# A hybrid encoder block: a second tile for the row of forget logs, second key copies read from PSUM, and four gate chunks moved from the forgetting attention into the dense stage

## The chip, the cores and the metric

The kernel runs on one core of a Trainium2 chip. The metric is the device time of one execution in microseconds, and a kernel is judged by the median of its runs. TensorE (PE) multiplies; VectorE (DVE), ScalarE (ACT) and GpSimd (POOL) do the element-wise work; SyncE (SP) and POOL issue the DMAs. PSUM, into which TensorE writes, has eight banks, one for each 128 x 512 float32 tile here.

## The reference

One residual block over 1024 tokens of width 1024, in float32: a normalization, one input projection split among three token mixers, sigmoid gates for each mixer and channel, an output projection; then a second normalization and a convolutional GLU. Cut to what matters here:

```python
z = rmsnorm(x, norm_mix_g) @ w_in
hq, hf, hi, hg, fq, fk, fv, ff, mq, gate_logits = split(z)
y_a = hgrn2(hq, hf, hi, hg)              # 4 heads, chunkwise recurrence
y_b = fox(fq, fk, fv, ff)                # forgetting attention, 8 heads of 64
y_c = cross_attention(mq, mem)           # 4 heads of 128, 256 memory tokens
gates = sigmoid(gate_logits)             # 3 branches x 1024 channels
merged = sum(gates[b] * (y[b] @ w_br[b]) for the three branches)
x = x + merged @ w_out
x = x + conv_glu(rmsnorm(x, norm_ffn_g))

def fox(q, k, v, f_logit):               # for each head
    Fc = cumsum(log_sigmoid(f_logit + f_bias))       # the row of forget logs
    s = rmsnorm(q) . rmsnorm(k) / 8 + Fc[t] - Fc[s]  # s <= t, blocks of 128 queries
    return softmax(s) @ v
```

## The kernel before

Every float32 product is made of three float32r products of a high and a low part (`mm3`, L112: high x high, high x low, low x high). The high part is a rounded copy (`cast`, on ACT), the low part the difference (on DVE); `split` does both.

The normalized input stands in SBUF by channels as `uh` and `ul` (8 tiles each). It is multiplied with the input weights in three ways:

- *Chunk by chunk* (`cm_chunk`, L154): 128 output channels by 1024 tokens, in two halves of 512, each 8 x 3 matmuls into one bank `pp`.
- *Two chunks at once* (`dense_unit`, L450): a Strassen-like scheme over blocks of 512 tokens and half of the depth, with sums of weight blocks (`s1` to `s4`) and sums of input blocks prepared once (`T1` to `T4`). Seven products of 4 x 3 matmuls give both chunks. `PAIRS` lists the pairs of chunks: first the four query chunks of the memory attention (12 to 15), then gate chunks.
- *Token by token block* (`token_major`, L580): 128 tokens by about 256 channels, where `uh` is the stationary side. It makes keys, queries and values for attention (`fox_proj`, `fox_values`) and the HGRN inputs (`hgrn_values`).

There are 24 gate chunks (3 branches x 8), in the order `ORDER`. Two are made while the input arrives, `NCOVER` = 2 before the dense units, `NPAIR` = 10 in the dense units, and the rest one by one during the attention by `gates_early`: `NFOX` says how many beside each of the first seven heads. A gate chunk is multiplied by the norm's factor into a `gt` tile (`gate`, L379; three `gt` tiles rotate), goes through a tanh, and is stored to DRAM (`gd`) by a DMA on SP. The branches fetch it from there later.

The forgetting attention runs by pairs of heads (`fox_proj`, `fox_prep`, then `fox_attn` for the first and for the second head):

- `fox_proj(p)` writes the tokens' keys and queries to `z`, squares them (`fsq`), sums, takes the power -1/2 on POOL and multiplies.
- `fox_prep(p)` (L736) transposes `z` on TensorE into a bank `ptr` and leaves the high and low parts of keys and queries in 64 of 128 partitions, and the keys a second time in the other 64, since one product has the high query in one half and the low query in the other. ACT makes the high part `kh`, DVE the low part `kl`; POOL copies both into the other half.
- `fox_attn(p, i)` (L771) loads the head's row of forget logs to all partitions (`nf`, one tile). For each 128 queries (`tb`, 0 to 7) TensorE makes the logits in `lg` banks; DVE adds the forget logs and takes the maximum (L800), after POOL has added the mask for the diagonal block (`nfm`, L789); ACT takes the exponential (L810); POOL divides (L812). The probabilities lie in `pt`, four tiles of 1024 columns that rotate, and `fsq` takes a turn among them. By pairs of `tb`, TensorE transposes the probabilities, ACT and DVE split them (`ph`, `pl`), and TensorE multiplies with the values into `po`; the two parts of the result are added in `yp` (L838, one tile) and stored by a DMA on SP.

The program is woven: `weave` advances several generators by their shares. The first head of pair `p` is woven with the projection of the next pair; the second with the gate chunks of `NFOX`; the last pair with `hgrn_values`. Attention instructions have a priority 300 instructions ahead (`ahead`, `AHEAD`). A planner then orders each engine's instructions, with its own estimate of their times; a tile of a rotating tag waits for the last use of the tile that it takes over, in the order of the program. After the last head comes the HGRN stage: `hgrn_prep` (L903) makes three chunks for a head, for the first head through `gt` tiles (L914), and `hgrn_mix` runs the recurrence.

Of the kernel before, what the change touches and what calls it, by code (L numbers as in the profile page):

```python
# [8 lines left out]
F32 = mybir.dt.float32  # L9
F32R = mybir.dt.float32r  # L10
AF = mybir.ActivationFunctionType
ALU = mybir.AluOpType
AX = mybir.AxisListType

P = 128
T = 1024
# [9 lines left out]


ORDER = [(br, j) for br in (1, 0, 2) for j in range(8)]
NCOVER, NPAIR = 2, 10
NFOX = [0, 3, 0, 3, 0, 3, 1]  # L30

_dense = [12, 13, 14, 15] + [16 + 8 * br + j for br, j in ORDER[4:4 + NPAIR]]
PAIRS = list(zip(_dense[0::2], _dense[1::2]))
# [37 lines left out]
def tile_block(ctx: ExitStack, tc: tile.TileContext, xT, memT, x_rows, mem_rows, vec, fbias, mats, hmask, w_cm, w_hi, w_fqk, w_fv,  # L71
# [46 lines left out]
    def cast(eng, out, in_):  # L118
        if eng is S:
            return S.copy(out, in_)  # L120
        elif eng is V:
            V.tensor_copy(out, in_)
        else:
            G.tensor_scalar(out, in_, 1.0, 0.0, ALU.mult, ALU.add)
# [251 lines left out]
    def gate_tile():  # L376
        return home["pool"].tile([P, HB], F32, tag="gt", name="gt", bufs=3)
# [221 lines left out]
    pools = {}  # L599
# [114 lines left out]
    def fox_proj(p):  # L714

        fox_z[p] = [None, None]

        def evac(tb, ps):
            n, b = tb // 4, tb % 4
            if b == 0:  # L720
                fox_z[p][n] = pq.tile([P, 4, 256], F32, tag="z", name=f"z{p}_{n}", bufs=2)
            z = fox_z[p][n]
            S.activation(z[:, b, :], ps, AF.Copy, scale=rt[:, tb:tb + 1])
            if b == 3:
                zz = z.rearrange("p b (h d) -> p (b h) d", d=64)
                sq = pools["pf"].tile([P, 16, 64], F32, tag="pt", name="fsq", bufs=4) if p else \
                    pm.tile([P, 16, 64], F32, tag="fsq", name="fsq")
                r = pq.tile([P, 16], F32, tag="fr", name="fr", bufs=2)
                S.activation(sq, zz, AF.Square)
                V.reduce_sum(r, sq, axis=AX.X)  # L730
                rstd_small(r, r, 64)
                V.tensor_mul(zz, zz, r.unsqueeze(2).to_broadcast([P, 16, 64]))

        yield from token_major(w_fqk[p], 256, evac)

    def fox_prep(p, after=None):  # L736
        kh = [pf.tile([P, T], F32R, tag=f"kh{i}", name=f"kh{i}_{p}", bufs=1 + i) for i in range(2)]
        qa = [pf.tile([P, T], F32R, tag=f"qa{i}", name=f"qa{i}_{p}", bufs=1 + i) for i in range(2)]
        kl = [pf.tile([P, T], F32R, tag=f"kl{i}", name=f"kl{i}_{p}", bufs=1 + i) for i in range(2)]
        for n in range(2):  # L740
            sl = slice(n * HB, (n + 1) * HB)
            z = fox_z[p][n]
            for what in range(2):
                gc = col(C_FK) if what == 0 else fqs
                ptr = ps_tr()
                with tc.issue_after(after.ins) if after is not None else nullcontext():
                    for b in range(4):
                        PE.transpose(ptr[:, b * P:(b + 1) * P], z[:, b, what * P:(what + 1) * P], ident)
                for i in range(2):
                    a = slice(64 * i, 64 * i + 64)  # L750
                    o = slice(64 * (1 - i), 64 * (1 - i) + 64)
                    if what == 0:
                        S.activation(kh[i][a, sl], ptr[a, :], AF.Copy, scale=gc[a, :])
                        V.scalar_tensor_tensor(out=kl[i][a, sl], in0=ptr[a, :], scalar=gc[a, :],
                                               in1=kh[i][a, sl].bitcast(F32), op0=ALU.mult, op1=ALU.subtract)
                        cast(G, kh[i][o, sl], kh[i][a, sl].bitcast(F32))
                        cast(G, kl[i][o, sl], kl[i][a, sl].bitcast(F32))
                    else:
                        S.activation(qa[i][a, sl], ptr[a, :], AF.Copy, scale=gc[a, :])
                        V.scalar_tensor_tensor(out=qa[i][o, sl], in0=ptr[a, :], scalar=gc[a, :],  # L760
                                               in1=qa[i][a, sl].bitcast(F32), op0=ALU.mult, op1=ALU.subtract)
        fox_sets[p] = [kh, kl, qa, None]
# [8 lines left out]
    def fox_attn(p, i):  # L771
        kh, kl, qa, _ = fox_sets[p]
        h = 2 * p + i
        a = slice(64 * i, 64 * i + 64)
        if h not in fox_vh:
            fox_vsplit(h)
        vhl = fox_vh[h]
        nf = pf.tile([P, T], F32, tag="nf", name="nf")
        SP.dma_start(nf, negFd[h:h + 1, :].partition_broadcast(P))
        for tp in range(4):  # L780
            pts = []
            for j in range(2):
                tb = 2 * tp + j
                ns = (tb + 1) * P
                tsl = slice(tb * P, (tb + 1) * P)
                pt = pf.tile([P, T], F32, tag="pt", name="pt", bufs=4)
                st = pf.tile([P, 4], F32, tag="st", name="st", bufs=4)
                nfm = pf.tile([P, P], F32, tag="nfm", name="nfm")
                G.tensor_tensor(nfm, nf[:, tsl], mskf, ALU.add)  # L789
                m = 0  # L790
                for s0 in range(0, ns, HB):
                    w = min(HB, ns - s0)
                    ps = ps_lg()
                    PE.matmul(ps[:, :w], qa[i][:, tsl], kh[i][:, s0:s0 + w], start=True, stop=False)  # L794
                    fox_sets[p][3] = PE.matmul(ps[:, :w], qa[i][:, tsl], kl[i][:, s0:s0 + w], start=False, stop=True)  # L795

                    d = w - P if s0 + w == ns else w
                    for lo, hi, bias in ((0, d, nf[:, s0:s0 + d]), (d, w, nfm)):
                        if lo < hi:
                            V.tensor_tensor_reduce(out=pt[:, s0 + lo:s0 + hi], in0=ps[:, lo:hi], in1=bias,  # L800
                                                   op0=ALU.add, op1=ALU.max, scale=1.0, scalar=-3e38,
                                                   accum_out=st[:, m:m + 1])
                            m += 1
                if m == 3:
                    V.tensor_tensor(st[:, 0:1], st[:, 0:1], st[:, 2:3], ALU.max)
                if m > 1:
                    V.tensor_scalar(st[:, 2:3], st[:, 0:1], st[:, 1:2], -1.0, ALU.max, ALU.mult)  # L807
                else:
                    V.tensor_scalar(st[:, 2:3], st[:, 0:1], -1.0, None, ALU.mult)
                S.activation(pt[:, :ns], pt[:, :ns], AF.Exp, bias=st[:, 2:3], accum_out=st[:, 3:4])  # L810
                V.reciprocal(st[:, 3:4], st[:, 3:4])  # L811
                G.tensor_scalar(pt[:, :ns], pt[:, :ns], st[:, 3:4], 0.0, ALU.mult, ALU.add)  # L812
                pts.append(pt)
                yield
            po = ps_po()
            for sp in range(tp + 1):
                ptr = ps_tr()
                w = 384 if sp == tp else 512
                for jj in range(2):
                    sb = 2 * sp + jj  # L820
                    ssl = slice(sb * P, (sb + 1) * P)
                    if sb <= 2 * tp:
                        PE.transpose(ptr[:, jj * 256:jj * 256 + P], pts[0][:, ssl], ident)
                        PE.transpose(ptr[:, jj * 256 + P:jj * 256 + 256], pts[1][:, ssl], ident)  # L824
                    else:
                        PE.transpose(ptr[:, 256:384], pts[1][:, ssl], ident)
                ph = pf.tile([P, HB], F32R, tag="ph", name="ph", bufs=2)
                pl = pf.tile([P, HB], F32R, tag="pl", name="pl", bufs=2)
                split(S, ph[:, :w], pl[:, :w], ptr[:, :w])
                for jj in range(2):  # L830
                    sb = 2 * sp + jj
                    last = sb == 2 * tp + 1
                    o = po[:, P:256] if last else po[:, 0:256]
                    src = slice(256, 384) if last else slice(jj * 256, jj * 256 + 256)
                    PE.matmul(o, vhl[:, sb, :], ph[:, src], start=(sb == 0), stop=False)  # L835
                    PE.matmul(o, vhl[:, sb, :], pl[:, src], start=False, stop=last)  # L836
                yield
            yp = pf.tile([64, 256], F32, tag="yp", name="yp")  # L838
            S.copy(yp, po[64:128, :256])
            V.tensor_add(yp, po[0:64, :256], yp)  # L840
            SP.dma_start(ybd[a, p, tp * 256:(tp + 1) * 256], yp)
            yield
# [812 lines left out]
```

## Time and profile before

| | us |
|---|---|
| median of 3 runs | 1734.2 |
| lowest and highest | 1732.5, 1734.95 |
| the profiled execution's own time | 1735.67 |
| its span, first to last instruction | 1733.9 |
| TensorE busy | 1714.0 |
| VectorE busy | 1144.5 |
| ScalarE busy | 808.3 |
| GpSimd busy | 322.8 |

The rows below come from the page of the profile and from views of its trace. A group is one line, engine and operation with its tiles (out<-in) and its count, then busy time, mean duration in ns, idle time of the engine just before it and what ended most of that. A row of the timeline has the start in us from the span's start, the duration, engine, line and operation. Matmuls are pipelined and their ends are modelled, so the pace of TensorE is read from starts, not from durations. PEld is the loading of weights, which overlaps. PEclk is the TensorE clock that was granted, as a share of full speed.

### The profile page before, as it was taken

The page shows a single profiled execution, that of the slowest core. Times are in us where ns is not written, and L with a number is a line of the kernel's source. Part 1 is how long each engine was busy: PE and PEld are TensorE (multiplying, and loading weights), DVE is VectorE, ACT ScalarE, POOL GpSimd, SP SyncE. Part 2 cuts the span into 40 slices and gives each one's busy share as a digit, 9 for nine tenths or more (in the row PEclk, how much of TensorE's full clock was granted, in tenths as well). Part 3 has the DMA queues.
Part 4 walks back from the last instruction along what each step waited for, and adds up shares of the span by engine and source line. Part 5 has one row for each costly group of instructions (what it writes and reads, how often), then busy time and mean ns, then how long its engine had stood idle before and what let it go on. Part 6 is the DMA issues. An engine that isn't in the chain of part 4 may idle for free.

```text
span 1733.9 us, 24255 instructions
## 1 busy us (share of the span) xinstructions
PE 1714.0 (99%) x8941; PEld 1452.6 (84%) x8941; DVE 1144.5 (66%) x2046; ACT 808.3 (47%) x1436; POOL 322.8 (19%) x417
## 2 busy tenths in 40 slices
PE   8999999999999999999989999999999999999998
PEld 6778899989898998888878888788888888888887
DVE  7656545665666564886856745987777787765654
ACT  8634346645454553776531333644334344433332
POOL 0100022443433331544210000211111111100000
PEclk9999999999999999999999999999999999999999
DMA  9533142221212111100336542565445345494772
GB/s 358 179 123 115 66 137 86 76 90 44 98 62 79 55 50 56 61 31 24 111 113 199 162 182 97 158 172 168 138 148 140 116 133 152 159 348 157 249 264 85
DMA packets 83207, 227.23 MB, mean 131 GB/s; under 512 B 9600, under 2 KB 12424, under 8 KB 83088
## 3 DMA queue, kind: packets, MB, share of 16 engines
q1 hardware_dynamic: 65040, 161.19, 26.8%
q0 software_dynamic: 18048, 64.50, 12.8%
q8 instruction: 70, 1.15, 0.3%
q14 instruction: 49, 0.40, 0.1%
HBM read 180.78 MB, written 67.93 MB: 143 GB/s over the span
## 4 chain that ended last, share of the span: by engine, by line
PE 96%; DMA 2%; DVE 1%; SPq 0%; issue 0%; ACT 0%; POOL 0%; DVEq 0%; POOLq 0%; ACTq 0%
PE pp L116 21%; PE pp L115 21%; PE pp L114 21%; PE lg L116 4%; PE lg L115 4%; PE lg L114 4%; PE tr L115 2%; PE tr L116 2%; PE tr L114 2%; PE po L836 1%; PE lg L795 1%; PE lg L794 1%; PE po L835 1%; PE po L116 1%; PE po L114 1%; PE po L115 1%
## 5 line engine op out<-in xcount | busy, mean ns | idle before, releaser
L116 PE MATMUL pp<-uh,wl 128*128 128x512 f32 x412 | 164.4, 399 | 0.0
L115 PE MATMUL pp<-ul,wh 128*128 128x512 f32 x412 | 164.4, 399 | 0.0
L114 PE MATMUL pp<-uh,wh 128*128 128x512 f32 x412 | 163.6, 397 | 0.0
L115 PE MATMUL pp<-wl,uh 128*128 128x256 f32 (+1 forms) x512 | 145.9, 286 | 0.0
L116 PE MATMUL pp<-wh,ul 128*128 128x256 f32 (+1 forms) x512 | 145.6, 285 | 0.0
L114 PE MATMUL pp<-wh,uh 128*128 128x256 f32 (+1 forms) x512 | 145.1, 285 | 0.0
L120 ACT CAST wh<-s 128x512 fp32r<-128x512 f32 x113 | 68.3, 619 | 157.7 <-PE pp L115 84.9
L120 ACT CAST wh<-raw 128x1024 fp32r<-128x1024 f32 (+2 forms) x76 | 67.6, 890 | 111.6 <-PE pp L115 95.5
L120 ACT CAST wh<-rw 128x512 fp32r<-128x512 f32 x87 | 53.2, 619 | 104.7 <-PE pp L115 62.1
L1300 POOL DMA_DIRECT2D rw<-in_w_up x44 | 24.2, 556 | 399.4 <-DVE wl L1193 178.4
L114 PEld LDWEIGHTS pp<-wh,uh 128*128 128x128 f32 x512 | 96.7, 189 | 1.2
L116 PEld LDWEIGHTS pp<-wh,ul 128*128 128x128 f32 x512 | 96.8, 189 | 0.9
L115 PEld LDWEIGHTS pp<-wl,uh 128*128 128x128 f32 x512 | 96.7, 189 | 0.9
L128 DVE TENSOR_TENSOR wl<-raw,wh 128x1024 fp32r<-128x1024 f32 (+2 forms) x75 | 78.1, 1041 | 28.8 <-ACT wh L120 28.3
L120 ACT CAST dwh<-wr 128x1024 fp32r<-128x1024 f32 (+1 forms) x41 | 40.1, 979 | 118.5 <-PE tr L115 39.7
L114 PEld LDWEIGHTS pp<-uh,wh 128*128 128x128 f32 x412 | 78.0, 189 | 15.7 <-ACT wh L120 0.3
L115 PEld LDWEIGHTS pp<-ul,wh 128*128 128x128 f32 x412 | 77.5, 188 | 15.8
L116 PEld LDWEIGHTS pp<-uh,wl 128*128 128x128 f32 x412 | 77.5, 188 | 15.7
L128 DVE TENSOR_TENSOR dwl<-wr,dwh 128x1024 fp32r<-128x1024 f32 (+1 forms) x41 | 46.3, 1129 | 34.0 <-ACT dwh L120 33.9
L810 ACT ACTIVATE pt<-pt,st 128x128 f32<-128x128 f32 (+3 forms) x64 | 49.7, 777 | 40.0 <-DVE st L807 33.1
L812 POOL TENSOR_SCALAR pt<-pt,st 128x128 f32<-128x128 f32 (+3 forms) x64 | 51.1, 798 | 78.0 <-DVE st L811 59.9
L120 ACT CAST ph<-tr 128x512 fp32r<-128x512 f32 (+1 forms) x80 | 41.7, 544 | 39.8 <-PE tr L824 17.6
(500 smaller groups left out, 5145.3 us busy)
## 6 DMA issues: line engine op xcount, KB each, us to landing
rw<-in_w_up POOLq DMA_DIRECT2D x44, 512.0 KB, 4.6
sd<-in_w_dn POOLq DMA_DIRECT2D x30, 512.0 KB, 5.9
br<-yd SPq DMA_DIRECT2D x30, 512.0 KB, 5.3
raw<-in_w_cm SPq DMA_DIRECT2D x26, 512.0 KB, 3.4
gd<-gt SPq DMA_DIRECT2D x48, 256.0 KB, 2.0
gt<-gd SPq DMA_DIRECT2D x48, 256.0 KB, 2.7
yd<-fc SPq DMA_DIRECT2D x44, 256.0 KB, 2.4
wr<-sd SPq DMA_DIRECT2D x20, 512.0 KB, 5.0
```

Source lines behind the costliest of these rows:

```text
L114: PE.matmul(ps, lh, rh, start=first, stop=False, skip_group_check=more)
L115: PE.matmul(ps, lh, rl, start=False, stop=False, skip_group_check=more)
L116: PE.matmul(ps, ll, rh, start=False, stop=last, skip_group_check=more)
L120: return S.copy(out, in_)
L128: return (sub or V).tensor_sub(l, src, h.bitcast(F32))
L794: PE.matmul(ps[:, :w], qa[i][:, tsl], kh[i][:, s0:s0 + w], start=True, stop=False)
L795: fox_sets[p][3] = PE.matmul(ps[:, :w], qa[i][:, tsl], kl[i][:, s0:s0 + w], start=False, stop=True)
L810: S.activation(pt[:, :ns], pt[:, :ns], AF.Exp, bias=st[:, 2:3], accum_out=st[:, 3:4])
L812: G.tensor_scalar(pt[:, :ns], pt[:, :ns], st[:, 3:4], 0.0, ALU.mult, ALU.add)
L835: PE.matmul(o, vhl[:, sb, :], ph[:, src], start=(sb == 0), stop=False)
L836: PE.matmul(o, vhl[:, sb, :], pl[:, src], start=False, stop=last)
L1300: late["raw"] = G.dma_start(raw[:, 2 * i:2 * i + 2, :], src[:, 2 * i:2 * i + 2, :])
```

## The change

Four things change.

1. `NPAIR` goes from 10 to 14: nine dense units in place of seven, so four gate chunks are made in pairs in the dense stage. `NFOX` goes from 0, 3, 0, 3, 0, 3, 1 to 0, 2, 0, 2, 0, 2, 0.
2. `nf` has two tiles, so the row of forget logs of a head can be loaded while the head before it still uses its own.
3. The copies of the keys in the other 64 partitions are made from PSUM, the high part by ACT and the low part by DVE; POOL's two copies are gone.
4. To make room, the four `pt` tiles become four tags with 5, 6, 7 and 8 blocks of 128 columns (`tb` % 4), `fsq` takes the widest of these (`pt3`), and `yp` takes a part of a gate tile (`gt`).

```diff
-NCOVER, NPAIR = 2, 10
-NFOX = [0, 3, 0, 3, 0, 3, 1]
+NCOVER, NPAIR = 2, 14
+NFOX = [0, 2, 0, 2, 0, 2, 0]
...
-                sq = pools["pf"].tile([P, 16, 64], F32, tag="pt", name="fsq", bufs=4) if p else \
+                sq = pools["pf"].tile([P, 16, 64], F32, tag="pt3", name="fsq") if p else \
...
-                        S.activation(kh[i][a, sl], ptr[a, :], AF.Copy, scale=gc[a, :])
-                        V.scalar_tensor_tensor(out=kl[i][a, sl], in0=ptr[a, :], scalar=gc[a, :],
-                                               in1=kh[i][a, sl].bitcast(F32), op0=ALU.mult, op1=ALU.subtract)
-                        cast(G, kh[i][o, sl], kh[i][a, sl].bitcast(F32))
-                        cast(G, kl[i][o, sl], kl[i][a, sl].bitcast(F32))
+                        for to in (a, o):
+                            S.activation(kh[i][to, sl], ptr[a, :], AF.Copy, scale=gc[a, :])
+                        for to in (a, o):
+                            V.scalar_tensor_tensor(out=kl[i][to, sl], in0=ptr[a, :], scalar=gc[a, :],
+                                                   in1=kh[i][a, sl].bitcast(F32), op0=ALU.mult, op1=ALU.subtract)
...
-        nf = pf.tile([P, T], F32, tag="nf", name="nf")
+        nf = pf.tile([P, T], F32, tag="nf", name="nf", bufs=2)
...
-                pt = pf.tile([P, T], F32, tag="pt", name="pt", bufs=4)
+                pt = pf.tile([P, (5 + tb % 4) * P], F32, tag=f"pt{tb % 4}", name="pt")
...
-            yp = pf.tile([64, 256], F32, tag="yp", name="yp")
+            yp = gate_tile()[:64, :256]
```

## The prediction

> **What bounds the kernel now.** I read the page first: busy time by engine and the chain that ended last.
>
> ```profile
> span 1733.9 us, 24255 instructions
> ...
> PE 1714.0 (99%) x8941; PEld 1452.6 (84%) x8941; DVE 1144.5 (66%) x2046; ACT 808.3 (47%) x1436; POOL 322.8 (19%) x417
> ...
> PE 96%; DMA 2%; DVE 1%; SPq 0%; issue 0%; ACT 0%; POOL 0%; DVEq 0%; POOLq 0%; ACTq 0%
> ```
>
> TensorE carries the chain, so the time is its work plus its holes. Next come the busy times by stretch: two dense units, the forgetting attention from the first to the last of its heads, the HGRN stage.
>
> ```profile
> core 0: us, PE busy (x) PEld busy (x) DVE busy (x) ACT busy (x) POOL busy (x), PEclk, DMA share, GB/s
> 155.00:194.00 39.00, 39.00 (x170) 31.56 (x169) 22.02 (x35) 15.87 (x28) 1.05 (x2) 1.00 0.24 83
> 337.00:690.00 353.00, 353.00 (x2334) 321.43 (x2332) 216.34 (x648) 180.00 (x352) 123.34 (x169) 1.00 0.19 65
> 700.00:910.00 210.00, 205.64 (x1171) 174.28 (x1170) 151.20 (x250) 122.92 (x298) 74.76 (x68) 0.98 0.20 65
> ```
>
> The attention has no hole: 353.00 of 353 us. No other engine is near its limit there (DVE 216 of 353). It is full only because it is fed with work that isn't attention: projections and gate chunks that run while a head waits for its softmax. The change takes part of this feed away. So there are two questions: what the dense stage saves, and whether the attention still fills the array.
>
> **Moving four gate chunks.** A dense unit makes two chunks of 1024 tokens with seven products of 4 x 3 matmuls, 84 in all. A plain chunk has 2 halves x 8 x 3 = 48, so two have 96. The first stretch holds two units, 168 matmuls and two cut by its ends: 39.00 / 168 = 0.2321 us each, at a clock of 1.00. Added: two units, 2 x 84 x 0.2321 = 39.0 us. Removed from the attention: 4 x 48 x 0.2321 = 44.6 us. Net, if both stages stay full: **-5.6 us**. The dense stretch has no hole, so I bound the added units by 0.4 us to either side. Other instructions of the four chunks move with them and lie beside TensorE in both places: DVE has 17 us free in those 39. On the queues, the weights move from SP to POOL. There four more issues wait, as the others do, for a buffer to come free, and nobody stands behind them: POOL is busy for 1.05 of those 39 us. SP loses four weight loads and issues the same gate results, earlier.
>
> **Is there slack in the attention?** I count the feed from the groups of that stretch (each row has two companions of the same count, give or take one), and the pace of the narrow matmuls from two rows of the timeline, twelve matmuls apart.
>
> ```profile
> L114 PE MATMUL pp<-wh,uh 128*128 128x256 f32 x289 | 81.7, 283 | 0.0
> ...
> L114 PE MATMUL pp<-uh,wh 128*128 128x512 f32 x204 | 80.6, 395 | 0.0
> ```
>
> ```profile
> 423.54 0.28 PE L114 MATMUL pp<-wh,uh 128*128 128x256 f32 x1
> ...
> 424.95 0.28 PE L114 MATMUL pp<-wh,uh 128*128 128x256 f32 x1
> ```
>
> Narrow: 1.41 / 12 = 0.1175 us, so 868 x 0.1175 = 102.0 us; wide: 611 x 0.2321 = 141.8 us. What is left, 109.2 us, is the eight heads' own work, 13.7 us each with the key transposes. A head now has 353 / 8 = 44.1 us of TensorE work; after, (353 - 44.6) / 8 = 38.6 us. Can a head be that quick? First matmul of the seventh head and of the eighth:
>
> ```profile
> 602.60 0.22 PE L794 MATMUL lg<-kh,qa 128*128 128x128 f32 x1
> ...
> 632.52 0.22 PE L794 MATMUL lg<-kh,qa 128*128 128x128 f32 x1
> ```
>
> That head took 29.9 us to the next one's start, without a hole. And it isn't the head that sets the pace. This is the tightest hand-over I found by pairing each difference (L128) with its value product (L836):
>
> ```profile
> 423.98 0.55 DVE L128 TENSOR_TENSOR pl<-tr,ph 128x384 fp32r<-128x384 f32 x1
> ...
> 426.38 0.36 PE L836 MATMUL po<-pl,vhl 128*128 128x256 f32 x1
> ```
>
> The operand was ready at 424.53, TensorE came at 426.38: 1.85 us late; in the other 79 it is later still. Heads wait for TensorE, not the reverse, and 5.5 us less per head is under four such hand-overs of ten. So I take no idle from the average.
>
> **Results through the gate ring.** `yp` now takes one of the three `gt` tiles, in program order with the gates. In a second head the order is yp0, g0, yp1, g1, yp2, g2, yp3, g3. So g0 takes the tile of the preceding head's third result, and g1 that of its own head's first. Until now gates ran far ahead:
>
> ```profile
> L114 PE MATMUL pp<-uh,wh 128*128 128x512 f32 x48 | 18.8, 392 | 0.0
> ...
> L381 DVE TENSOR_TENSOR gt<-pp,rx 128x512 f32<-128x512 f32 x6 | 4.2, 692 | 11.9 <-PE pp L116 11.9
> ```
>
> These are the groups of 354 to 399.5 us: all three gate chunks of the second head (3 x 48 matmuls, six evacuations) ran under the first. After, three PSUM banks of 24 matmuls (72, or 16.7 us) can run before the ring lets a result out. An evacuation that waits holds DVE's queue, behind it the softmax's reductions. I cost this at 0, since 13.7 + 16.7 = 30.4 us is above the 29.9 shown; the other end is the first rival.
>
> The ring also reaches the end. Prep of the first HGRN head uses gate tiles, and feeds the last head from 649 to 690 us (first row; then DVE's timeline, and the landing of the store of `yp`):
>
> ```profile
> L114 PE MATMUL pp<-uh,wh 128*128 128x512 f32 x44 | 17.4, 396 | 0.0
> ```
>
> ```profile
> 690.59 0.42 DVE L840 TENSOR_TENSOR yp<-po,yp 64x256 f32<-64x256 f32 x1 [5.30 <-ACT yp L839]
> 691.12 1.29 DVE L915 TENSOR_TENSOR gt<-pp,rx 128x512 f32<-128x512 f32 x2
> ```
>
> ```profile
> DMA to landing us min/median/max: 1.9/2.0/4.2
> ```
>
> Before, 131 matmuls (44 + 44 + 43) went in until 690 us, through three banks and the three tiles. After, the third tile is the last result's: free at 690.59 + 0.42 + about 0.4 of issue + 2.0 = 693.4 instead of 691.12, and until then five halves fit, 120 matmuls. Short by 11 x 0.2321 = 2.5 us, late by 2.3 us. Bounds 0 to 4.8 us. With fewer fillers the head ends sooner and asks for fewer of them, so I take **+1.2 us**, half of the first.
>
> **Key copies, forget row, tiles.** The instructions on the key tile (min, median and max in ns):
>
> ```profile
> L753 ACT ACTIVATE kh<-tr,cv x16: 669/683/687, 329.2 to 581.1; 64x512 fp32r<-64x512 f32 x16
> L754 DVE SCALAR_TENSOR_TENSOR kl<-tr,cv,kh x16: 742/750/760, 329.9 to 581.9; 64x512 fp32r<-64x512 f32 x16
> L124 POOL TENSOR_SCALAR kh<-kh x16: 615/617/1531, 332.6 to 581.9; 64x512 fp32r<-64x512 f32 x16
> ```
>
> POOL loses these 16 casts and as many of the low parts, about 20 us; ACT gets 16 x 0.68 = 10.9 and DVE 16 x 0.75 = 12.0. DVE would stand at about 228 less the gates' part, of 308: covered. A bank is read 1.43 us longer, 16 times: 0 while TensorE has feed, at worst 11.4 us in all; near 0, as each lies under 38 us of other work. The row of forget logs cost this:
>
> ```profile
> POOL nfm L789 <- DMA nf<-negFd: 15.4, 5, 4.9
> ```
>
> POOL waited, TensorE did not: 0, and up to 4.9 us of chain gained per head if feed runs short. The load goes a head earlier on SP, so stores behind it no longer wait for its tile.
>
> The probability tiles still rotate by four. But `fsq` now always takes the fourth: the second square of a projection waits until the head's last tile has been transposed, with ACT's queue behind it. Then come square, reduction, power and product:
>
> ```profile
> L729 ACT ACTIVATE fsq<-z x7: 1057/1060/1061, 326.4 to 555.2; 128x1024 f32<-128x1024 f32 x7
> L730 DVE TENSOR_REDUCE fr<-fsq x7: 1207/1220/1221, 327.7 to 556.3; 128x16 f32<-128x1024 f32 x7
> ```
>
> ```profile
> L133 POOL TENSOR_TENSOR fr<-fr,mhalf x7: 2912/2914/3268, 329.2 to 559.0; 128x16 f32<-128x16 f32 x7
> L732 DVE TENSOR_TENSOR z<-z,fr x7: 1208/1476/1809, 333.7 to 562.6; 128x1024 f32<-128x1024 f32 x7
> ```
>
> 1.06 + 1.22 + 2.91 + 1.48 = 6.7 us before the next keys can be transposed, and the whole second head lies between: 0; three times 6.7 if that cover were gone.
>
> **Sum.** -5.6 + 1.2 = -4.4 us. The profiled execution took 1735.67 us (span 1733.9), 1.5 above the median of 1734.2. It would become 1731.3, the median **1729.8**.
>
> **Rivals.** *Slower: the ring starves the first heads.* At heads one, three and five gates can't run ahead; if a head's chain takes longer than 30.4 us, TensorE idles by the difference, three times. Above 31.9 us (3 x 1.47) the 4.4 are gone. At 34 us, a third of the way from 29.9 to the present 44.1, it is 3 x 3.6 = 10.8 us: 1740.6. For it speaks that one quick head proves little, and that the others took longer; against it that all 80 hand-overs have TensorE late. A hole may cost more than itself:
>
> ```profile
> 889.00:894.00 5.00, 1.08 (x7) 0.85 (x6) 2.91 (x6) 2.37 (x7) 1.01 (x1) 0.86 0.34 105
> 894.00:898.00 4.00, 3.89 (x19) 3.59 (x17) 0.82 (x2) 0.77 (x3) 0.00 (x0) 0.50 0.00 0
> 898.00:902.00 4.00, 3.67 (x19) 3.34 (x20) 1.82 (x5) 0.96 (x2) 0.00 (x0) 0.82 0.01 2
> ```
>
> After 3.9 us idle in the first stretch the clock is 0.50, then 0.82: 4 x 0.50 + 4 x 0.18 = 2.7 us lost. For a hole of 3.6 us no row shows this, and I leave it out. [...]
>
> *No change: the gain is given back at the end.* The last head pays the full 4.8 us: -0.8, 1733.4. For it: the feed there is nearly used up already (131 of 144 matmuls). Against: the two shortages overlap.
>
> *More: HGRN begins with other feed and loses its idle time,* 210 - 205.64 = 4.4 us on top: 1725.4. Nothing in the change aims at it.
>
> *It doesn't do what it says.* If a planner's order lets no forget row load early, nothing is lost: TensorE never waited for it.
>
> **Numbers.** Forecast 0.58, no change 0.17, slower 0.20, more 0.05. A measurement here can tell 0.2%, 3.5 us, from no change; forecast and "more" are faster by over that: faster 0.63, same 0.17, slower 0.20. The range goes from 1726, the full 5.6 and half of HGRN's idle time, to 1740, just short of the slower rival's price: about 0.15 is left out.
>
> **What would show it.** Right: nine dense units 19.5 us apart; the first attention matmul some 39 us later; TensorE nearly full through the eight heads in about 308 us; no `nfm` wait for a DMA; wide matmuls with `uh` fewer by 192 as plain chunks. Wrong: TensorE waiting in the attention for PSUM evacuations (`pp`) or for `pl`, `gt` waiting for a store, a clock under 1.00 there, or dense units further apart.

## The result, and the profile after

The changed kernel takes **1760.8 us** (median; 1760.1 to 1762.1) against 1734.1 (1732.5 to 1735.0) for the kernel before: a ratio of 1.0157, 95% interval 1.0142 to 1.0172. It is 26.6 us slower; the forecast was 4.4 us faster. The profiled execution took 1760.97 us, its span is below (the page: span, busy times by engine, the granted clock in 40 slices, the chain that ended last).

```profile
span 1759.2 us, 24218 instructions
...
PE 1716.7 (98%) x8917; PEld 1451.5 (83%) x8917; DVE 1165.7 (66%) x2086; ACT 827.9 (47%) x1468; POOL 302.7 (17%) x389
...
PEclk9999999998999899999999999999999999999999
...
PE 93%; DVE 3%; DMA 2%; ACT 1%; issue 1%; POOL 1%; SPq 0%; POOLq 0%; DVEq 0%; ACTq 0%
```

TensorE's share of the chain fell from 96% to 93%, DVE's rose from 1% to 3%, and two slices of the clock, 396 to 440 and 572 to 616 us, show 8. Now the busy times by stretch: four dense units, the attention, the HGRN stage; first of after, then the last two of before, in the same windows (columns as in the prediction).

```profile
155.00:233.00 78.00, 78.00 (x338) 63.15 (x337) 44.71 (x71) 31.73 (x57) 3.15 (x6) 1.00 0.29 96
340.00:720.00 380.00, 351.23 (x2411) 323.92 (x2410) 243.94 (x700) 216.59 (x427) 127.74 (x159) 0.96 0.18 58
740.00:950.00 210.00, 209.85 (x1160) 175.55 (x1159) 141.87 (x234) 107.86 (x252) 63.14 (x59) 1.00 0.26 85
```

```profile
340.00:720.00 380.00, 380.00 (x2456) 342.90 (x2455) 238.81 (x676) 202.56 (x399) 141.67 (x178) 1.00 0.20 66
740.00:950.00 210.00, 205.64 (x1117) 173.23 (x1116) 142.62 (x238) 97.88 (x238) 54.68 (x53) 0.98 0.31 98
```

The dense units cost what was forecast: 39.00 us for two. HGRN lost 4.2 us of idle time. The loss is in the attention: 380.00 - 351.23 = 28.8 us idle where there was none, and a clock of 0.96. With the 5.6 us saved in the dense stage that is 28.8 - 5.6 - 4.2 = 19.0; the span grew by 25.3. The low clock explains most of the 6.3 that are left: added up over stretches of 1 us, it takes 8.0 us from TensorE's busy time in 330 to 740 us, where before loses nothing, and behind 740 us nothing, where before loses 2.7. TensorE's waits name the places (line waited for: us in total, times, longest):

```profile
PE tr L824 <- DVE kl L757: 15.8, 3, 5.4
PE tr L748 <- DVE z L732: 6.0, 1, 6.0
PE tr L748 <- DVE kl L757: 5.9, 2, 4.6
```

(One line is inserted ahead of the key copies, so line numbers behind L750 are one higher than before.) All three are at the key preparation between the first and the second head of a pair, three times in the kernel. The first of them, in the timeline of TensorE, of ACT, and of DVE:

```profile
426.89 1.94 PE L748 MATMUL tr<-ident,z 128*128 128x128 f32 x8 [5.97 <-DVE z L732]
434.05 0.45 PE L824 MATMUL tr<-ident,pt 128*128 128x128 f32 x1 [5.22 <-DVE kl L757]
```

```profile
428.01 1.38 ACT L755 ACTIVATE kh<-tr,cv 64x512 fp32r<-64x512 f32 x2 [3.13 <-PE tr L748]
429.42 0.68 ACT L760 ACTIVATE qa<-tr,fqs 64x512 fp32r<-64x512 f32 x1
430.96 1.38 ACT L755 ACTIVATE kh<-tr,cv 64x512 fp32r<-64x512 f32 x2 [0.86 <-DVE kl L757]
...
437.87 0.37 ACT L840 COPY gt<-po 64x256 f32<-64x256 f32 x1 [0.44 <-PE po L837]
```

```profile
429.43 1.50 DVE L757 SCALAR_TENSOR_TENSOR kl<-tr,cv,kh 64x512 fp32r<-64x512 f32 x2 [1.90 <-ACT kh L755]
...
432.37 1.53 DVE L757 SCALAR_TENSOR_TENSOR kl<-tr,cv,kh 64x512 fp32r<-64x512 f32 x2 [0.79 <-ACT kh L755]
...
438.21 0.69 DVE L381 TENSOR_TENSOR gt<-pp,rx 128x512 f32<-128x512 f32 x1
```

Three things are to be seen. ACT and DVE read the key bank in turns, four times: from 428.01 to 433.90, 5.9 us. The next head's transposes (L824) want that bank and start 0.15 us later. And no gate matmul fills the 5.97 and 5.22 us: the gates' evacuation (L381) comes at 438.21, directly behind the next head's first result (L840 at 437.87), which now stands in the same ring; until then their `pp` banks are full. TensorE had run 72 gate matmuls (three banks of 24) by 412.9 us and runs no projection or gate matmul again before 439.03. Then the clock (busy times by stretch):

```profile
424.00:427.00 3.00, 0.11 (x1) 0.14 (x2) 2.92 (x5) 0.86 (x3) 1.66 (x2) 0.57 0.01 2
427.00:434.00 7.00, 1.83 (x8) 1.35 (x8) 4.29 (x7) 4.09 (x6) 0.30 (x1) 0.50 0.00 0
434.00:440.00 6.00, 5.95 (x27) 5.32 (x28) 5.61 (x21) 3.49 (x8) 1.69 (x3) 0.66 0.00 0
```

In the last row TensorE is busy again, at 0.66: 6 x 0.34 = 2.0 us lost on top of the hole.

### The profile page after: what moved, and what is told of

It reads as the page before. It is cut to its first block, busy times and chain, and to the rows that moved or that the text cites. A ratio compares the mean times of both kernels' runs of the same rounds, so it can differ in the third digit from the quotient of the medians.

```text
span 1759.2 us, 24218 instructions
## 1 busy us (share of the span) xinstructions
PE 1716.7 (98%) x8917; PEld 1451.5 (83%) x8917; DVE 1165.7 (66%) x2086; ACT 827.9 (47%) x1468; POOL 302.7 (17%) x389
## 3 DMA queue, kind: packets, MB, share of 16 engines
q8 instruction: 70, 1.15, 0.3%
## 4 chain that ended last, share of the span: by engine, by line
PE 93%; DVE 3%; DMA 2%; ACT 1%; issue 1%; POOL 1%; SPq 0%; POOLq 0%; DVEq 0%; ACTq 0%
PE pp L116 20%; PE pp L115 20%; PE pp L114 20%; PE lg L116 4%; PE lg L115 4%; PE lg L114 4%; PE tr L115 2%; PE tr L116 2%; PE tr L114 2%; PE lg L796 1%; DVE kl L757 1%; PE po L837 1%; PE lg L795 1%; PE tr L824 1%; PE po L116 1%; PE po L836 1%
## 5 line engine op out<-in xcount | busy, mean ns | idle before, releaser
L120 ACT CAST wh<-s 128x512 fp32r<-128x512 f32 x121 | 73.0, 619 | 167.7 <-PE pp L115 83.4
L116 PE MATMUL pp<-uh,wl 128*128 128x512 f32 x356 | 143.1, 402 | 0.0
L115 PE MATMUL pp<-ul,wh 128*128 128x512 f32 x356 | 141.9, 399 | 0.0
L114 PE MATMUL pp<-uh,wh 128*128 128x512 f32 x356 | 141.2, 397 | 0.0
L120 ACT CAST wh<-raw 128x1024 fp32r<-128x1024 f32 (+2 forms) x72 | 63.5, 881 | 105.4 <-PE pp L115 91.0
L120 ACT CAST wh<-rw 128x512 fp32r<-128x512 f32 x93 | 56.8, 619 | 108.9 <-PE pp L115 67.8
L128 DVE TENSOR_TENSOR wl<-raw,wh 128x1024 fp32r<-128x1024 f32 (+2 forms) x71 | 72.9, 1027 | 29.1 <-ACT wh L120 28.7
L114 PEld LDWEIGHTS pp<-uh,wh 128*128 128x128 f32 x356 | 67.5, 190 | 14.2 <-ACT wh L120 0.3
L115 PEld LDWEIGHTS pp<-ul,wh 128*128 128x128 f32 x356 | 67.0, 188 | 14.3
L116 PEld LDWEIGHTS pp<-uh,wl 128*128 128x128 f32 x356 | 67.0, 188 | 13.8
```

What stands on the lines that cost most here:

```text
L114: PE.matmul(ps, lh, rh, start=first, stop=False, skip_group_check=more)
L115: PE.matmul(ps, lh, rl, start=False, stop=False, skip_group_check=more)
L116: PE.matmul(ps, ll, rh, start=False, stop=last, skip_group_check=more)
L128: return (sub or V).tensor_sub(l, src, h.bitcast(F32))
```

## The experiments

Theory A, after the result: three edits cost time, each for itself. The moved chunks take feed that the heads need; the copies from PSUM hold a bank; the ring keeps the gates from running ahead. Rivals: the square on the probability tile, the load on ACT and DVE, or only the three together. Each comparison is with the kernel before, on the same chip. Where two of the other kernels are compared, their medians can come from different chips, between which the kernel before differs by up to 1.2 us.

| kernel | us (range) | ratio to before, 95% |
|---|---|---|
| changed kernel | 1760.8 (1760.1-1762.1) | 1.0157 (1.0142-1.0172) |
| e1 chunks moved, nothing else | 1745.1 (1744.3-1746.0) | 1.0064 (1.0049-1.0079) |
| e2 all but the move | 1763.5 (1761.4-1764.0) | 1.0167 (1.0151-1.0182) |
| e3 changed, no ring, one forget row | 1753.8 (1752.2-1756.1) | 1.0111 (1.0094-1.0127) |
| e4 changed, own square, one forget row | 1762.0 (1761.0-1763.7) | 1.0162 (1.0147-1.0177) |
| e6 changed, copies by POOL | 1748.1 (1747.0-1749.4) | 1.0079 (1.0062-1.0096) |
| e7 moved + copies from PSUM | 1756.3 (1755.1-1756.9) | 1.0127 (1.0112-1.0142) |
| e10 moved, gates held back | 1764.7 (1764.5-1765.9) | 1.0177 (1.0162-1.0192) |
| e11 two chunks moved | 1738.9 (1737.0-1741.4) | 1.0030 (1.0020-1.0040) |
| e13 copies from PSUM alone | 1742.9 (1741.4-1743.5) | 1.0049 (1.0034-1.0064) |
| e14 ring and tiles alone | 1749.5 (1747.5-1750.9) | 1.0087 (1.0072-1.0102) |
| e15 moved + copies from SBUF | 1744.6 (1744.2-1746.9) | 1.0062 (1.0047-1.0077) |
| e16 moved, third z, results over tiles | 1785.3 (1782.9-1786.1) | 1.0291 (1.0274-1.0308) |
| e17 twelve chunks in the attention | 1731.4 (1729.8-1734.4) | 0.9985 (0.9975-0.9995) |
| e18 moved, results over tiles | 1777.2 (1776.1-1777.5) | 1.0246 (1.0230-1.0261) |
| e19 six chunks as 1, 2, 3 | 1750.1 (1747.3-1751.8) | 1.0089 (1.0074-1.0104) |
| e20 ten chunks as 2, 3, 4, 1 | 1736.4 (1735.2-1738.0) | 1.0015 (1.0006-1.0025) |
| e21 fourteen chunks in the attention | 1734.8 (1733.3-1737.0) | 1.0002 (0.9992-1.0011) |
| e22 tiles and square alone | 1733.2 (1731.8-1735.6) | 0.9996 (0.9987-1.0006) |

### The three edits apart

**e1, the move alone.**

```diff
-NCOVER, NPAIR = 2, 10
-NFOX = [0, 3, 0, 3, 0, 3, 1]
+NCOVER, NPAIR = 2, 14
+NFOX = [0, 2, 0, 2, 0, 2, 0]
```

> The kernel before with nothing but the four gate chunks moved (14 chunks in pairs, two per second head); tiles and key copies as before. Too little feed (the attention can't do without the four chunks): 1750 or more, TensorE idle in the attention for over 25 us. Tile theories (the square's place or the gate ring makes the stalls): 1728 to 1732, that is 5.6 us of dense saving less 0 to 3, hardly any TensorE wait in the attention. Bank theory (key copies): the same 1728 to 1732.

11 us slower, between the two forecasts, with the tiles and copies of before. Two stretches of its attention, by busy times:

```profile
498.00:510.00 12.00, 9.29 (x62) 7.59 (x62) 10.31 (x33) 8.49 (x19) 7.99 (x10) 1.00 0.12 40
604.00:632.00 28.00, 21.69 (x135) 17.90 (x134) 20.82 (x79) 16.13 (x36) 12.36 (x20) 0.94 0.09 27
```

In each the feed is used up: from 606 to 632 us no projection or gate matmul runs at all, and the end of the sixth head and the first half of the seventh show their bare chain, 21.69 busy of 28. In all 9.4 us are idle among the heads, and 5.7 more at the start of HGRN (701 to 725 us), where before has none.

**e2, all but the move** (the changed kernel with the two lines above undone).

> The changed kernel with the chunks where they were (10 in pairs, three per second head): only tiles, forget row and key copies change. If feed that is there hides these edits: 1733 to 1737. If the gate ring or the copies cost whatever the amount of feed: 1745 to 1755, with the same 5.5 us waits of the next head's transposes for the key copies, three times.

Not faster than the changed kernel: 1763.5, above both forecasts. With the full feed the holes are the same ones:

```profile
PE tr L824 <- DVE kl L757: 16.5, 3, 5.6
...
PE tr L748 <- DVE z L732: 6.0, 1, 6.0
```

So feed doesn't help where the ring keeps it from running, and beside ring and copies the move costs nothing: with it the time is 2.7 us lower, which the intervals of the two kernels don't tell apart.

**e6 and e7, the copies.** e6 is the changed kernel with POOL's copies put back, e7 the moved chunks with the copies from PSUM.

> The changed kernel with POOL making the second key copies from SBUF again; all else as changed. Copy theory (ACT and DVE read one bank in turns for 6 us, and no feed covers it): 1745 to 1751, that is 11 us less than the changed kernel, as the copies added 11 to the moved chunks alone. Ring theory: 1756 or more.

> The kernel before with the four gate chunks moved and the key copies made from PSUM; probability tiles, square, yp and forget row as before. Bank theory (the banks of the key transposes are read longer, so the next head's transposes wait for the copies): 3 x 5.5 us of wait, 1742 to 1748. Square and ring theories: 1728 to 1732. Too little feed: 1750 or more.

They are worth 12.6 us in the changed kernel (1760.8 - 1748.1) and 11.2 beside the moved chunks (1756.3 - 1745.1). e6 is where the copy theory had it; e7 is 8 us above the bank theory's range, which had left out what the move costs by itself. TensorE's wait for the same bank in e6:

```profile
PE tr L823 <- DVE kl L754: 7.3, 3, 2.4
```

2.4 us a time instead of 5.3.

**e3 and e4, ring and square.** In e3 the results have a tile of their own, in e4 the square has; in both, `nf` has one tile, since there is no room for two.

```diff
-            yp = gate_tile()[:64, :256]
+            yp = pf.tile([64, 256], F32, tag="yp", name="yp")
```

> The changed kernel with yp in a tile of its own again, so gate results share their ring with nothing; to make room the forget row has one tile. The square stays in the widest probability tile. Ring theory (feed can't run ahead, because gate results wait for yp's tiles): 1728 to 1735, the waits before the key transposes and before the next head's transposes gone or filled. Square theory (the second square waits for the head's last transposes, which makes the keys late): 1752 to 1761, three holes of 5 us before the key transposes remain.

> The changed kernel with the square (fsq) in a tile of its own, and one tile for the forget row to make room; yp stays in the gate ring. Square theory: 1728 to 1738, the wait of the key transposes for z gone. Ring theory: 1752 to 1761, TensorE still without feed while the keys are made.

Square and second forget row together are worth nothing (1762.0 against 1760.8, just above the ring theory's range): with the square early, the key transposes wait for `kl` all three times, 12.0 us in sum, where the changed kernel waits 6.0 for `z` once and 5.9 for `kl` twice. The ring is worth 8 us here (1762.0 - 1753.8, or 7.0 from the changed kernel, with the second forget row in it). e3's time lies in the range of the square theory, but the holes of that theory are gone: TensorE waits for no `z`. The gates run ahead again, with evacuations (L381) at 397.75, 405.67, 412.63 and 420.37 us, where the changed kernel has its first at 438.21.

### Each edit by itself, and what it costs by

**e13, the copies alone, and e15, the same number of copies from SBUF.** e13 is the kernel before with the changed copies. In e15 (beside the moved chunks) ACT and DVE make the second copies from the first ones:

```diff
                         S.activation(kh[i][a, sl], ptr[a, :], AF.Copy, scale=gc[a, :])
                         V.scalar_tensor_tensor(out=kl[i][a, sl], ...)
-                        cast(G, kh[i][o, sl], kh[i][a, sl].bitcast(F32))
-                        cast(G, kl[i][o, sl], kl[i][a, sl].bitcast(F32))
+                        if i == 1:
+                            for ii in range(2):
+                                ...
+                                cast(S, kh[ii][oo, sl], kh[ii][aa, sl].bitcast(F32))
+                                cast(V, kl[ii][oo, sl], kl[ii][aa, sl].bitcast(F32))
```

> The kernel before, with the second key copies taken from PSUM by ACT and DVE instead of being made by POOL, and nothing else of the change (all ten gate chunks stay among the attention heads). Theory 'the copies cost by holding the bank': each of the eight key banks is read for about 5.5 us instead of 2.4, whatever the feed, and the next head's transposes and the second half of the key transposes wait for it: 1734 + 11 = about 1745 us, with waits of some 5 us of TensorE for kl in the list of waits. Rival 'the copies cost only when the feed is short': with the full feed the wide matmuls cover the longer bank, and the time is 1734 to 1737 us, the holes of 5 us missing. (The copies cost 11.2 us on top of the moved chunks, and 12.6 us on top of the ring and the moved chunks.)

> The moved chunks and the old tiles, with the second key copies made by ACT (kh) and DVE (kl) as in the change, but from the first copies in SBUF, after both halves of the bank have been read. ACT and DVE get the same number of extra instructions as with the copies from PSUM; the bank is read only as long as before. Theory 'the bank is held too long': most of the 11.2 us between the moved chunks alone (1745.1) and the moved chunks with the copies from PSUM (1756.3) is gone, 1744 to 1748 us, and the waits of TensorE for kl are 2 to 3 us long. Rival 'the load on ACT and DVE': the time stays at 1754 to 1757 us, and the next half's copies queue behind the SBUF copies.

e15 decides it: 1744.6, what the moved chunks cost without any copies moved (1745.1), and not 1756.3. ACT and DVE have the extra instructions, and they are free; the bank isn't. Its timeline at the same place, ACT and then DVE:

```profile
432.93 0.69 ACT L753 ACTIVATE kh<-tr,cv 64x512 fp32r<-64x512 f32 x1 [1.50 <-PE tr L748]
433.65 0.62 ACT L120 CAST kh<-kh 64x512 fp32r<-64x512 f32 x1
...
435.00 0.68 ACT L753 ACTIVATE kh<-tr,cv 64x512 fp32r<-64x512 f32 x1
```

```profile
433.65 0.74 DVE L754 SCALAR_TENSOR_TENSOR kl<-tr,cv,kh 64x512 fp32r<-64x512 f32 x1 [2.32 <-ACT kh L753]
434.43 0.42 DVE L122 CAST kl<-kl 64x512 fp32r<-64x512 f32 x1
...
435.79 0.76 DVE L754 SCALAR_TENSOR_TENSOR kl<-tr,cv,kh 64x512 fp32r<-64x512 f32 x1
```

The bank is read from 432.93 to 436.55: 3.6 us instead of 5.9, although copies have slipped in between the halves. e13 fits neither of its theories well: 8.3 us slower, but TensorE waits for no `kl`. With all the feed the longer banks are covered, and the cover is paid for: feed runs earlier and is missing at the end. This is read from the trace, not shown by a run: in 620 to 640 us, in the seventh head, e13 has 62 feed matmuls, before has 97; and of e13's 9.5 us idle, 6.0 stand at the end of the attention and the start of HGRN (690 to 730 us).

**e14 and e22, the new tiles with and without the ring.** e14 is the kernel before with results in the ring, the second forget row, tiles by length and the square on the fourth; e22 has only the last two.

```diff
-                pt = pf.tile([P, T], F32, tag="pt", name="pt", bufs=4)
+                pt = pf.tile([P, (5 + tb % 4) * P], F32, tag=f"pt{tb % 4}", name="pt")
...
-                sq = pools["pf"].tile([P, 16, 64], F32, tag="pt", name="fsq", bufs=4) if p else \
+                sq = pools["pf"].tile([P, 16, 64], F32, tag="pt3", name="fsq") if p else \
```

> The kernel before with the new tiles alone: results through the gate ring, probability tiles by length, second home of the forget row, square on the fourth probability tile; the key copies stay with POOL, the ten gate chunks stay in the attention. Theory 'three separate prices' (the ring, the copies and the moved chunks each cost for themselves): all but the move came to 1763.5 us, and the copies are worth 12 of that, so this kernel stands at about 1751 us, with TensorE waiting 5 to 6 us for z at a key preparation and no gate matmul running while it waits. Rival 'the ring hurts only together with short feed or long banks': within 4 us of the kernel before, 1734 to 1738 us, and then the 30 us of all-but-the-move belong mostly to the copies.

> The kernel before with the probability tiles by length and the square on the fourth of them, and nothing else: results in their own tile, one row of forget logs, POOL copies, ten chunks in the attention. With the results through the gate ring and the second row as well it was 1749.5 us; with results over the probability tiles and the moved chunks 1777. Theory 'the results' stores hold what others need' (the ring's 15 us are the ring's): 1733 to 1736 us. Rival 'the tiles by length or the square on them': 1745 to 1750 us, with the square of a second half late and TensorE waiting for z.

Tiles and square cost nothing (0.9996); ring and second row together cost the 15 us. The second row came out at nothing beside the square in e4, so I put the 15 down to the ring. The gates bear this out: in e22 the six evacuations of the second head's gates stand at 359.88 to 396.60 us, and e14 has none before 397.17. In e14 the holes of the changed kernel are there with the full feed and POOL's copies, shorter where the bank is free sooner:

```profile
376.00:394.00 18.00, 9.61 (x56) 8.09 (x55) 12.78 (x28) 9.38 (x17) 11.58 (x14) 0.81 0.04 13
```

```profile
PE tr L823 <- DVE kl L754: 6.4, 3, 2.4
...
PE tr L748 <- DVE z L732: 5.7, 1, 5.7
```

**e10, gates held without a ring:** the moved chunks alone, each gate half issued after those logits of the head that precede it in the program.

```diff
-        weave(..., (gates_early(NFOX[2 * p + 1]), 2 * NFOX[2 * p + 1], FOX_LATE))
+        weave(..., (beside(p, gates_early(NFOX[2 * p + 1])), 2 * NFOX[2 * p + 1], FOX_LATE))
...
+            with tc.issue_after(fox_sets[p][3].ins):
+                next(gen)
```

> The chunks moved as in the change, tiles and copies as before, and each gate half beside a second head held until the head's logits that precede it in the program have been issued, so that the feed isn't drawn a head early. Availability theory (the feed is enough but is used up before the next projection may begin): 1729 to 1736, the dry patch of TensorE at the end of the third and sixth head gone. Amount theory (too little feed wherever it lies): 1743 to 1750, as with the chunks moved and nothing else.

I had thought that feed which is drawn early is drawn too early, and that holding it back would spread it. That fell: 1764.7 is above both forecasts and 19.6 us slower than e1. Held gates leave the key preparation bare, as the ring does:

```profile
411.00:440.00 29.00, 22.21 (x120) 18.38 (x119) 19.38 (x57) 16.21 (x30) 12.25 (x19) 0.82 0.05 14
```

I read it as the ring's price by another means: a gate that runs ahead isn't wasted, it covers the preparation.

### Amount of feed, or its place

**e11, e17 and e21, the dose; e19 and e20, the place.** Only the two lines of numbers differ: `NPAIR` 12, 8, 6 with `NFOX` 0, 3, 0, 2, 0, 2, 1 (e11), 0, 4, 0, 4, 0, 4, 0 (e17) and 0, 5, 0, 4, 0, 4, 1 (e21); 14 with 0, 1, 0, 2, 0, 3, 0 (e19); 10 with 0, 2, 0, 3, 0, 4, 1 (e20).

> The kernel before with two chunks moved instead of four (12 in pairs; 3, 2, 2 per second head and 1 beside the seventh). Amount theory, linear: half of 11, 1739 to 1741. If the cost sets in only past two chunks: 2.8 us less than before, 1730 to 1733.

> The kernel before with the dose turned round: twelve gate chunks among the attention heads instead of ten (four beside each second head of the first three pairs, none in the seventh), one dense unit less. Theory 'amount of feed': the attention of before has no hole that more feed could fill (TensorE's excess there is about 0), so each chunk moved back costs the difference in price between the two places, 5.6 / 4 = 1.4 us each, and the time is 1734 + 2.8 = about 1737 us. Rival 'every chunk moved out costs 2.8 us, every one moved in gains as much' (the two and four moved chunks went +4.7 and +11): about 1729 us.

> The dose turned round further: fourteen gate chunks among the attention heads (five, four, four beside the second heads and one in the seventh), two dense units less than before. Twelve came to 1731.4 us (2.2 under the kernel before), with no excess of TensorE left in 360-720 us. Theory 'amount': with no hole left to fill, two chunks more only cost the difference in price, at 1.4 us each: 1733 to 1736 us. Rival 'each chunk moved in goes on gaining': 1728 to 1730 us.

> The moved chunks with the six that remain spread otherwise: one, two and three beside the second heads of the first three pairs instead of two, two and two. Same work, same tiles. Theory 'drawn too early': the sixth head, which has no feed from 606 to 632 us with two each, gets a third chunk, and the second head, which has feed to spare, loses one: 1737 to 1741 us instead of 1745. Rival 'amount': the hole moves to the head that gave its chunk, 1744 to 1748 us.

> The kernel before with its ten gate chunks spread two, three, four and one instead of three, three, three and one. Before has no holes in the attention, so both theories expect no change: 1733 to 1736 us; if the second head needs its three chunks, some us more.

With 6, 8, 10, 12 and 14 chunks among the heads the times are 1745.1, 1738.9, 1734.2, 1731.4, 1734.8. Against the kernel before on the same chip they are 11.0, 5.5, 0, -2.2 and 1.1 us. Below ten each chunk that is taken away costs 2.7 to 2.8 us; above twelve each one added costs 1.7, close to the 5.6 / 4 = 1.4 us by which the dense stage makes it cheaper. So from six to ten it is the amount. The step from ten to twelve is of another kind. I had expected 1737 for e17, since I saw no hole left to fill in 360 to 720 us, and there was none: TensorE is full there in both. Yet e17 is at 1731.4, faster than both kernels (0.9985, 0.9975 to 0.9995). Its gain lies behind the heads: TensorE is busy for 209.85 us of 740 to 950, 4.2 more than before (e17's two stretches, then a wait of before).

```profile
340.00:720.00 380.00, 380.00 (x2419) 341.12 (x2419) 228.84 (x639) 197.91 (x392) 132.23 (x167) 1.00 0.20 69
740.00:950.00 210.00, 209.85 (x1125) 175.19 (x1124) 138.12 (x229) 91.89 (x216) 48.55 (x48) 1.00 0.32 102
```

```profile
PE tr L1067 <- ACT o L1064: 3.9, 1, 3.9
```

This pause in HGRN is in before, e20 and e22, all with ten chunks, and is missing with twelve and fourteen, but also in the changed kernel with its six. No run shows what takes it away. So the least at twelve belongs to this pause, not to the attention.

Place matters too, the other way than I thought: chunks shifted from the second head to the sixth cost 5 us (e19 against e1, above both of its forecasts) and 2.8 (e20). The sixth head is fuller then, and the end of the third and the start of the fourth go bare: 30 feed matmuls in 480 to 500 us, where e1 has 88.

**e16 and e18, a third tile for z.** Moved chunks, tiles by length; to make room, results are written over the first probability tile of their pair, which is dead by then. e16 has a third `z`, e18 has not.

```diff
-            yp = pf.tile([64, 256], F32, tag="yp", name="yp")
+            yp = pts[0][:64, :256]
...
+                fox_z[p][n] = pools["pf"].tile([P, 4, 256], F32, tag="zf", ...) if (2 * p + n) % 3 == 2 else \
```

> The moved chunks with the old POOL copies and one row of forget logs; a third tile for z (the projections' evacuated halves), for which room is made by the probability tiles by length and by writing each result over the first probability tile of its pair, which is dead by then; the square on the fourth probability tile. Nothing of the gate ring. Theory 'the next projection is blocked': with the moved chunks alone (1745.1 us) the feed is missing at 498-510 us since the next projection can't start before the key preparation frees its tile; a third tile lets 96 of its matmuls run there, and the hole of some 10 us closes: about 1735 to 1738 us. Rival 'the amount of feed': the work that fills the one hole is missing in the next (the stretch without feed in the sixth head grows as much), and the time stays at 1743 to 1747 us.

> The kernel with the third z, without the third z: moved chunks, probability tiles by length, square on the fourth of them, results written over the first probability tile of their pair, z in two tiles. If the 40 us by which that kernel was slower than the moved chunks alone come from the results over the probability tiles (a tile is free only when its result is stored) or from the square's place, this one stands at 1780 to 1790 us as well. If they come from the third z (projections drawn earlier still, the heads from 600 us on without feed), this one stands at 1743 to 1750 us like the moved chunks alone.

Both theories of e16 fell (1785.3); e18 says why: most of it is the price of making room (1777.2, 32 us above e1 and just under the first of its forecasts). A probability tile isn't free before its result is stored, and DVE waits there:

```profile
DVE pt L800 <- DMA ybd<-pt: 21.8, 17, 3.0
```

The third `z` adds 8 us to that. Beside such holes I can't say what it would do alone; whether the blocked projection costs anything by itself stays open.

## Why the prediction was wrong, step by step

- **Moving four gate chunks, -5.6:** right. Two units take 39.00 us in the new place as in the old, and e21 with e17 gives 1.7 us a chunk for the difference, where 1.4 was forecast.
- **Is there slack in the attention? "I take no idle from the average":** the step that failed first, by 16.6 us (e1: +11.0 where -5.6 was forecast). The sums were right, 38.6 us of work for a head that can do with 29.9. But the feed is a stock that heads draw on as soon as they wait, not a share for each. The prediction had the row for it: three gate chunks of the second head had run under the first by 399.5 us. Read so, the question is when the stock runs out, and in e1 that is first at 497 us, and again at 606. The hand-over of 1.85 us spoke against a change of this size only for a TensorE that is fed.
- **Results through the gate ring, 0:** wrong by some 15 us (e14 with e22). The 72 matmuls of cover ran as counted, but TensorE had used them up by 412.9 us, ahead of the key preparation and not in it. The rival named the mechanism and the place, the gates no longer ahead at the second heads. It priced it by a head's whole chain against 30.4 us of cover; the holes are at the key preparation (in e14 one of 5.7 us and three of up to 2.4). Its 3.6 us a hole, three times, are 10.8; with the 2.7 us that the clock took in the prediction's row put on each, though no run shows that for such a hole, they make 18.9; that this is near the 15 is luck.
- **Key copies, 0 while TensorE has feed:** wrong by 8 (e13) to 12.6 us (e6), and POOL's relief was worth nothing. Its worst case was also summed wrongly: 16 times 1.43 is 22.9, not 11.4; the trace has 5.89 us for a bank that took 3.02 before, so 8 x 2.87 = 23.0. The prediction looked at DVE's total (covered, and e15 confirms it) and never asked who needs the bank next: the next head's transposes, which have two `tr` banks. ACT and DVE read it in turns, so each added pair of reads holds it for the sum of both, 0.68 + 0.75 us; in the stretch shown, 428.01 to 433.90, no two of these reads overlap. The waits here are for the whole bank: at 430.96 ACT waits 0.86 us for reads that lie in the other 64 partitions. No run here tried a wait for each half.
- **Forget row, tiles, square on `pt3`, 0:** right (e22 0.9996, e4). "The whole second head lies between" was the wrong reason for it: in the changed kernel TensorE does wait 6.0 us for that `z`, but where the square is early it waits as long for `kl`.
- **The last head's end, +1.2:** not measured by itself; behind the heads the changed kernel is 4.2 us better off in HGRN, as the rival *more* had it; what took HGRN's pause away stays open.

The prices don't add up: 11 + 8 + 15 = 34 against 26.6; I take it that the holes overlap. Ring and copies together cost 30.2 us with all the feed (e2, against 1733.4 on its chip), so beside them the move costs nothing more.

## What to carry to other kernels

A stage that shows no idle time because other work fills it has no slack that an average could show: ask where the filler is used up, and take the filler away only while the first bare stretch is still covered. Before giving an engine another read of a PSUM bank, or another producer a place in a ring of tiles, ask who takes over that bank or tile next, and whether TensorE has anything else it may run then; the load on the engines says little. The cheap test is the dose in both directions: here two chunks the other way gained 2 us, though behind the heads and not in the attention.

## What the runs showed of the hardware

The clock fell in holes shorter than the 3.9 us of the prediction's row. In e1, after 2.21 us without a matmul (TensorE's timeline, then the clock in two stretches):

```profile
704.43 0.80 PE L114 MATMUL pp<-uh,wh 128*128 128x512 f32 x1 [2.21 <-DVE gt L915]
```

```profile
704.20:704.40 0.20, 0.00 (x0) 0.00 (x0) 0.20 (x2) 0.00 (x0) 0.20 (x1) 0.88 0.00 0
705.00:708.00 3.00, 3.00 (x9) 2.36 (x8) 0.64 (x3) 0.64 (x2) 2.91 (x3) 0.54 0.86 297
```

It falls at 704.35 and is back at about 707.8, which costs 1.7 us. Another fall in this trace is at 619.02, behind 3.01 us without a matmul.

How long it stays low, by the clock of the two kernels' traces, differs: in the changed kernel the falls are at 424.41, 513.16 and 591.66 us, and the clock is 0.50 for 13.65, 6.82 and 13.65 us; in the kernel before it is 0.50 for 3.41 us from 237.24 and for 6.83 us from 892.60, the fall in the prediction's row. Nor was TensorE idle throughout ahead of them: in the 4 us before each it was busy for 0.51, 1.15 and 1.90 us, and for 3.13 and 1.05 in the kernel before. How much work is enough to keep the clock, these traces don't show.
